# Two first copies given to VectorE, one feed-forward tile and one half tile moved in TensorE's order: a decoder layer on one Trainium2 core

## The chip, the cores and the metric

The kernel runs on one core of one Trainium2 chip. The metric is the device time of one execution in microseconds. TensorE is called PE here, VectorE DVE, ScalarE ACT, GpSimd POOL, and SyncE, which only issues transfers, SP. Each of them takes its instructions from its own queue, in order.

## The reference, cut to what matters

One decoder layer over 512 positions of width 1024: a norm, a combined projection, two attention branches merged by gates, an output projection, and then the part that this change touches, a second norm and a feed-forward block:

```
merged = gates[:, :, 0] * (y_a @ w_branch_a[l]) + gates[:, :, 1] * (y_b @ w_branch_b[l])
x = x + merged @ w_out[l]
h2 = rmsnorm(x, mlp_norm_g[l])
x = x + jnp.square(jax.nn.relu(h2 @ w_ff1[l])) @ w_ff2[l]      # w_ff1 1024x4096, w_ff2 4096x1024
return rmsnorm(x, final_norm_g)
```

## The kernel before

Each float32 product is made of three matmuls on PE: both operands are split into a high part (hi, ACT copies it, rounded) and the rest (lo, DVE or POOL subtracts), and hi·hi, hi·lo and lo·hi are added up in PSUM (`mm3`, L141 to L143). So each operand tile costs an ACT copy and then a subtraction, and the third matmul of a product needs the lo part of the left-hand tile.

Only PE's order is written out by hand. The order on ACT, DVE, POOL and SP comes from a scheduler that places each instruction by its own model of when its inputs are there. What the program text says about these four engines is therefore not yet their order.

**Start.** 52 tiny matmuls (`NWARM`, L160) run while the first inputs are loaded.

**Norm and start of the feed-forward.** The output projection (`out_proj`) goes over four blocks b of 128 positions. For each, the normed block xg is turned by eight PE transpositions (L875) and split by ACT (h2h, L876) and DVE (h2l, L877); that is `h2_block(b)`. For the last block, PE first runs the first halves (positions 0 to 255) of the tiles `ff1(0)` to `ff1(2)`, 24 matmuls each, then `h2_block(3)`, then the second halves. At the end of the transpositions the memory of the norm's tiles comes free, and the tiles that the second feed-forward product loads into (B, T) lie there.

**Feed-forward.** `ff1(f)` is one tile of 128 hidden units: 24 matmuls of 512 columns into a PSUM tile pt (two buffers), then ACT relu (z, L913) and square (z, L914). The second product goes in 8 groups g of four such tiles. Groups 0 to 6 multiply 2x2 block matrices by Strassen's scheme in Winograd's form, with 7 products per group (k = 0 to 6). `pair(g, k)` is one product, 2 x 6 matmuls on PE. Its left operand `as` is made by `put_a` (hi on ACT L953, lo on DVE L954) from the z tiles or from their sums S1 to S4 (DVE, L939). Its right operand `b` is made by `put_b` (hi on ACT L961, lo on DVE L962) from a loaded block (B11, B21, B22: `raw`, L923) or from a sum of blocks (T1 to T4: `tsum`). A T is loaded by SP (L928), and then POOL issues a second transfer that adds another block onto it (L929). T1 and T3 add a block from the weights, T2 adds T3 (so it waits for T3's landing), and T4 adds T2. The weights of ff1 tiles are loaded into `wraw` (L112) and split into whi (ACT, L119) and wlo (DVE, L121).

The products go to accumulators: `acc` (DVE, L985 or L983), and U and V, which collect products 0 and 2. In group 0 U and V have no contents yet and are copied from PSUM (L989), afterwards added to (L991). The order of PE in group 0 is ff1(3), ff1(4), pair(0,0), pair(0,1), ff1(5), pair(0,2), pair(0,3), pair(0,4), ff1(6), and so on; ff1(3) gives the second half of z1, the left operand of pair(0,1). The four PSUM tiles pl are used in turn, so pair(0,4) writes into those that pair(0,2) filled.

**End.** Group 7 is a plain product. In group 6 (`plain`), `last_put(j)` makes its left operand `al` (L999 on ACT, L1000 on DVE), `last_sums` joins U, V and acc, and `gfin`, the final norm's gains, is loaded into o (L1182 on SP) and scaled by ACT (L1183).

Of the kernel before, what the change touches and what calls it, by code (L numbers as in the profile page):

```python
# [14 lines left out]
AF = mybir.ActivationFunctionType  # L15
# [27 lines left out]
    return ap.to_broadcast(shape)  # L43


NWARM = 52
OHB = 12


def body(nc, tc, ctx, a, out, dbg=lambda name, ap: None):  # L50
    pe, dve, act, pool, sp = nc.tensor, nc.vector, nc.scalar, nc.gpsimd, nc.sync
# [19 lines left out]
    def utile(i, dt, name):  # L71
        return u_p.tile([128, 4, S], dt, tag=f"u{i}", name=name)
# [8 lines left out]
    def pa_tile():  # L81
        return psA.tile([128, S], F32, tag="pa", name="pa")

    def pl_tile():
        return psL.tile([128, S], F32, tag="pl", name="pl")

    def pt_tile():
        return psT.tile([128, NB, 128], F32, tag="pt", name="pt")
# [43 lines left out]
    def use(key, ahead=2):  # L132
        i = seq.index(key)
        for k in seq[i:i + ahead + 1]:
            pre(k)
        return W[key]

    def mm3(ps, parts):
        n = len(parts)
        for i, (lh, ll, rh, rl) in enumerate(parts):  # L140
            pe.matmul(ps, lh, rh, start=(i == 0), stop=False)  # L141
            pe.matmul(ps, lh, rl, start=False, stop=False)  # L142
            pe.matmul(ps, ll, rh, start=False, stop=(i == n - 1))  # L143
# [14 lines left out]
    pw = pa_tile()  # L158
    for _ in range(NWARM):
        pe.matmul(pw[:, 0:128], warmb, warmb, start=True, stop=True)  # L160
# [10 lines left out]
    k = 0  # L171
# [157 lines left out]
    for j in range(3):  # L329
# [9 lines left out]
        if j == 1:  # L339
# [12 lines left out]
            for j in range(2):  # L352
                t = t_p.tile([128, S], F32, tag="s2k", name="iqf", bufs=4)
# [155 lines left out]
    for b in range(NB):  # L509
        sl = slice(b * 128, (b + 1) * 128)  # L510
        for e in range(2):
            p = pl_tile()[:, :384]
# [40 lines left out]
    for j in range(4):  # L553
# [3 lines left out]
        p = pl_tile()  # L557
        cs = slice(128 * j, 128 * j + 128)
        mm3(p, [(ukh[:, cs], ukl[:, cs], zkh, zkl)])
        t = t_p.tile([128, S], F32, tag="s2k", name="kf", bufs=4)  # L560
# [10 lines left out]
        p = pl_tile()  # L571
# [75 lines left out]
    for t in range(0, 32 + BL, 2):  # L647
# [5 lines left out]
        h1, j = divmod(t - BL, 4)  # L653
# [161 lines left out]
    for m in range(NK):  # L815
# [4 lines left out]
        for br in (1, 0):  # L820
            yh, yl = (yah, yal) if br == 0 else (ybh, ybl)
            p = pl_tile()
# [47 lines left out]
    def h2_block(b):  # L870
        tk = slice(b * 128, (b + 1) * 128)
        for e in range(2):
            pt = pt_tile()
            for k in range(4):
                pe.transpose(pt[:, k], xg[b][:, (4 * e + k) * 128:(4 * e + k + 1) * 128], ident)  # L875
            act.activation(h2h.t[e][:, :, tk], pt, AF.Copy)  # L876
            dve.tensor_tensor(h2l.t[e][:, :, tk], pt, h2h.t[e][:, :, tk].bitcast(F32), op=ALU.subtract)  # L877
# [21 lines left out]
    def ff1_mm(p, f, lo=0, hi=S):  # L899
        wh_, wl_ = W["ff1", f]  # L900
        mm3(p[:, lo:hi], [(wh_[:, k], wl_[:, k], h2h[k][:, lo:hi], h2l[k][:, lo:hi]) for k in range(NK)])

    def ff1(f, p=None):
        g, i = divmod(f, 4)
        j, q = divmod(i, 2)
        if p is None:
            use(("ff1", f), min(2, 31 - f))
            p = pt_tile().rearrange("p a b -> p (a b)")
            ff1_mm(p, f)
        if q == 0:  # L910
            Z[g, j] = z_p.tile([128, 2, S], F32, tag=f"z{j}", name=f"z{j}", bufs=1)
        z = Z[g, j][:, q]
        act.activation(z, p, AF.Relu)  # L913
        act.activation(z, z, AF.Square)  # L914
# [6 lines left out]
    def raw(g, key):  # L921
        r = RAW[g, key] = wt_p.tile([128, 2, 512], F32, tag="raw", name=key, bufs=3)
        sp.dma_start(r, wsrc(g, key))  # L923

    def tsum(g, key):
        t = TT[g, key] = wt_p.tile([128, 2, 512], F32, tag="t", name=key, bufs=3)
        x, y = {"T1": ("B11", "B12"), "T3": ("B12", "B22"), "T2": ("B11", "T3"), "T4": ("B21", "T2")}[key]
        sp.dma_start(t, wsrc(g, x))  # L928
        pool.dma_start(t, TT[g, y] if y[0] == "T" else wsrc(g, y), accum_op=ALU.add)  # L929

    def asum(g, key):
        z0, z1 = Z[g, 0], Z[g, 1]
        t0, t1 = slice(0, 256), slice(256, 512)
        x, y, op = {"S1": (z0[:, :, t1], z1[:, :, t1], ALU.subtract),
                    "S2": (SS.get((g, "S1")), z0[:, :, t0], ALU.subtract),
                    "S3": (z0[:, :, t0], z0[:, :, t1], ALU.subtract),
                    "S4": (z1[:, :, t0], SS.get((g, "S2")), ALU.add)}[key]
        t = SS[g, key] = z_p.tile([128, 2, 256], F32, tag="s", name=key, bufs=3)
        dve.tensor_tensor(t, x, y, op=op)  # L939
# [17 lines left out]
    def put_b(g, k):  # L957
        key = ORDER[k][1] if g < NG - 1 else LASTB[k]
        x = (RAW if key[0] == "B" else TT)[g, key]
        t = bs_p.tile([128, 2, 2, 512], F32R, tag="b", name="b", bufs=NBS)  # L960
        act.activation(t[:, 0], x, AF.Copy)  # L961
        dve.tensor_tensor(t[:, 1], x, t[:, 0].bitcast(F32), op=ALU.subtract)  # L962
        BS[g, k] = (t[:, 0], t[:, 1])
# [3 lines left out]
    copied = {}  # L967

    def unit(g, k, m, cuts=(0, 512)):
        p = pl_tile()  # L970
        ah, al = AS[g, "op", k]
        bh, bl = BS[g, k]
        ms = slice(m * 128, (m + 1) * 128)
        for lo, hi in zip(cuts, cuts[1:]):
            c = slice(lo, hi)
            mm3(p[:, c], [(ah[:, q, ms], al[:, q, ms], bh[:, q, c], bl[:, q, c]) for q in range(2)])
            i, n = BLOCK.get(k, (0, 0))
            b = 2 * i + m
            cs = slice(512 * n + lo, 512 * n + hi)
            if k in BLOCK:  # L980
                t = acc[:, b, cs]
                if k == 5:
                    dve.tensor_tensor(t, t, p[:, c], op=ALU.subtract)  # L983
                else:
                    dve.tensor_tensor(t, p[:, c], t, op=ALU.add)  # L985
            t = {0: U, 2: V, 3: U}.get(k)
            if t is not None:
                if g == 0 and k != 3:
                    copied[k] = act.activation(t[:, m], p, AF.Copy)  # L989
                else:  # L990
                    dve.tensor_tensor(t[:, m], p[:, c], t[:, m], op=ALU.add)  # L991

# [3 lines left out]
    def last_put(j):  # L996
        t = utile(j, F32R, "al")
        hi, lo = t[:, 0:2], t[:, 2:4]
        act.activation(hi, Z[NG - 1, j], AF.Copy)  # L999
        dve.tensor_tensor(lo, Z[NG - 1, j], hi.bitcast(F32), op=ALU.subtract)  # L1000
        AS[j] = (hi, lo)
# [25 lines left out]
    def pair(g, k):  # L1027
        for m in range(2):
            unit(g, k, m)
# [3 lines left out]
    def group(g):  # L1033
        nxt = g + 1
        plain = nxt == NG - 1

        def nb():
            if bq:
                put_b(*bq.pop(0))

        def raws():
            for key in ("B11", "B21", "B12" if plain else "B22"):
                raw(nxt, key)

        if g == 0:
            put_a(g, 2)
            asum(g, "S4")
            ff1(4 * nxt)
            nb()
            tsum(0, "T4")  # L1050
            pair(g, 0)
            put_a(g, 3)
            pair(g, 1)
            with tc.issue_after(copied[0].ins):
                nb()
            put_a(g, 4)
            ff1(4 * nxt + 1)
            put_a(nxt, 0)
            nb()
            pair(g, 2)  # L1060
            raws()
            nb()
            nb()
            for key in ("T1", "T3", "T2"):
                tsum(nxt, key)
        else:
            pair(g, 0)
            raws()
            put_a(g, 2)
            asum(g, "S4")  # L1070
            ff1(4 * nxt)
            nb()
            pair(g, 1)
            nb()
            if not plain:
                for key in ("T1", "T3", "T2"):
                    tsum(nxt, key)
            put_a(g, 3)
            pair(g, 2)
            nb()  # L1080
            put_a(g, 4)
            ff1(4 * nxt + 1)
            if not plain:
                put_a(nxt, 0)
        put_a(g, 5)
        pair(g, 3)
        nb()
        put_a(g, 6)
        pair(g, 4)
        nb()  # L1090
        if plain:
            raw(nxt, "B22")
        else:
            tsum(nxt, "T4")
        ff1(4 * nxt + 2)
        if plain:
            last_put(0)
        pair(g, 5)
        nb()
        ff1(4 * nxt + 3)  # L1100
        if not plain:
            asum(nxt, "S1")
            asum(nxt, "S2")
        pair(g, 6)
        nb()
        if plain:
            last_put(1)
            last_sums()
        else:
            asum(nxt, "S3")  # L1110
            put_a(nxt, 1)
# [33 lines left out]
    for j in range(3):  # L1145
        use(("ff1", j), 2 - j)
        p0.append(pl_tile())
        ff1_mm(p0[j], j, 0, 256)
    h2_block(3)
    for j in range(3):  # L1150
        ff1_mm(p0[j], j, 256, S)
    m_st.close()
# [23 lines left out]
    for g in range(NG - 1):  # L1176
        group(g)
# [54 lines left out]
```

## Time and profile before

| what | value |
|---|---|
| time, median of 3 runs (lowest to highest) | 707.0 us (706.18 to 708.35) |
| time of the profiled execution | 708.5 us |
| its span in the trace | 706.8 us |
| PE busy | 689.6 us, 98% of the span |
| DVE, ACT, POOL busy | 72%, 51%, 27% |

The profiled execution's own time is 1.7 us above its span, which is what lies around the traced instructions, and 1.5 us above the median. Times in rows are microseconds from the start of the span. In a row of the timeline the first number is the start, the second the duration, then engine, line, operation, tiles and shape; in brackets at the end stands the idle time of that engine before the row, and what ended it. Matmuls overlap, so their pace is read from start to start.

### The profile page before, as it was taken

Reading aid. Unit: us, or ns where it says so; the run is one execution under the profiler, and the core shown is the slowest. Engines: PE = TensorE matmul, PEld = TensorE weight load, DVE = VectorE, ACT = ScalarE, POOL = GpSimd, SP = SyncE. Lnnn points to the kernel's source line nnn. Section 1 sums busy time; section 2 is a strip of 40 time slices with the busy share of each in tenths; the row PEclk is TensorE's granted clock in tenths of the full one; section 3 lists DMA queues with packets and bytes.
Section 4 is the critical chain, followed back from the end, with each engine's and each line's share of the span. In section 5 each row is a group of like instructions: output and inputs, shape, how many; then the busy total and the mean of one; then the engine's idle time right before and its main releaser. Section 6 shows DMA issues by size and latency. Waiting matters only on the chain.

```text
span 706.8 us, 10176 instructions
## 1 busy us (share of the span) xinstructions
PE 689.6 (98%) x3671; PEld 557.7 (79%) x3672; DVE 509.5 (72%) x936; ACT 360.9 (51%) x623; POOL 191.0 (27%) x235
## 2 busy tenths in 40 slices
PE   9999999999999999999999979999999999999996
PEld 7879788768865777888889768888888888888875
DVE  6487899999999765674323856958595776859643
ACT  6466767654735445761114755454354535444333
POOL 2305387665156540230011010101010011000132
PEclk9999999999999999999999999999999999999999
DMA  8632532112221117972009896878768786750012
GB/s 309 239 112 91 125 116 80 46 46 79 101 75 45 47 47 285 309 270 89 0 1 309 221 258 188 220 227 196 195 181 213 174 215 184 196 120 30 31 49 101
DMA packets 41587, 102.88 MB, mean 146 GB/s; under 512 B 4352, under 2 KB 5248, under 8 KB 41536
## 3 DMA queue, kind: packets, MB, share of 16 engines
q1 hardware_dynamic: 34848, 86.47, 36.1%
q0 software_dynamic: 5824, 14.68, 12.1%
q10 hardware_dynamic: 864, 1.08, 0.4%
q8 instruction: 29, 0.48, 0.3%
q14 instruction: 22, 0.18, 0.1%
HBM read 87.66 MB, written 6.29 MB: 133 GB/s over the span
## 4 chain that ended last, share of the span: by engine, by line
PE 77%; DVE 12%; DMA 5%; issue 2%; ACT 2%; POOL 1%; SPq 0%; POOLq 0%; ACTq 0%; DVEq 0%
PE pl L141 10%; PE pl L143 10%; PE pl L142 10%; PE pt L142 7%; PE pt L141 7%; PE pt L143 7%; PE pl L237 3%; PE pl L239 3%; PE pl L238 3%; DVE nmx L590 2%; DVE oh L714 2%; DMA T<-T 2%; PE pl L848 2%; PE pl L846 2%; PE pl L847 2%
## 5 line engine op out<-in xcount | busy, mean ns | idle before, releaser
L119 ACT ACTIVATE whi<-wraw 128x1024 fp32r<-128x1024 f32 (+1 forms) x71 | 74.6, 1051 | 92.4 <-PE pt L142 74.3
L121 DVE TENSOR_TENSOR wlo<-wraw,whi 128x1024 fp32r<-128x1024 f32 (+1 forms) x60 | 73.7, 1230 | 53.0 <-ACT whi L119 52.1
L141 PE MATMUL pt<-h2h,whi 128*128 128x512 f32 x232 | 90.3, 389 | 0.0
L142 PE MATMUL pt<-h2l,whi 128*128 128x512 f32 x232 | 90.3, 389 | 0.0
L143 PE MATMUL pt<-h2h,wlo 128*128 128x512 f32 x232 | 90.2, 389 | 0.0
L141 PE MATMUL pl<-b,as 128*128 128x512 f32 x196 | 77.3, 394 | 3.7 <-ACT V L989 3.7
L143 PE MATMUL pl<-b,as 128*128 128x512 f32 x196 | 76.8, 392 | 0.1
L142 PE MATMUL pl<-b,as 128*128 128x512 f32 x196 | 76.9, 392 | 0.0
L962 DVE TENSOR_TENSOR b<-T,b 128x1024 fp32r<-128x1024 f32 x28 | 34.2, 1221 | 28.3 <-ACT b L961 28.3
L961 ACT ACTIVATE b<-T 128x1024 fp32r<-128x1024 f32 x28 | 29.6, 1057 | 42.5 <-PE pl L143 15.3
L142 PEld LDWEIGHTS pt<-h2l,whi 128*128 128x128 f32 x232 | 43.6, 188 | 9.1
L141 PEld LDWEIGHTS pt<-h2h,whi 128*128 128x128 f32 x232 | 43.5, 188 | 9.0
L143 PEld LDWEIGHTS pt<-h2h,wlo 128*128 128x128 f32 x232 | 43.5, 188 | 9.0
L929 POOL DMA_DIRECT2D T<-wff x14 | 17.2, 1244 | 116.6 <-DVE V L991 40.0
L714 DVE TENSOR_SCALAR oh<-posbc,thr 128x400 bf16<-128x400 f32 (+31 forms) x128 | 45.6, 408 | 3.9 <-PE pl L735 3.9
L141 PEld LDWEIGHTS pl<-b,as 128*128 128x128 f32 x196 | 37.2, 190 | 12.1 <-ACT V L989 4.2
L237 PE MATMUL pl<-hh,whi 128*128 128x512 f32 x112 | 44.8, 400 | 0.0
L595 POOL TENSOR_SCALAR pra<-pra,rs 128x400 f32<-128x400 f32 (+31 forms) x32 | 35.1, 1109 | 35.2 <-DVE rs L594 35.1
L239 PE MATMUL pl<-hh,wlo 128*128 128x512 f32 x112 | 43.7, 390 | 0.0
L238 PE MATMUL pl<-hl,whi 128*128 128x512 f32 x112 | 43.7, 390 | 0.0
L143 PEld LDWEIGHTS pl<-b,as 128*128 128x128 f32 x196 | 37.1, 189 | 8.2 <-DVE as L954 0.5
L142 PEld LDWEIGHTS pl<-b,as 128*128 128x128 f32 x196 | 37.2, 190 | 8.1 <-DVE b L962 0.4
(324 smaller groups left out, 1683.7 us busy)
## 6 DMA issues: line engine op xcount, KB each, us to landing
wraw<-wff SPq DMA_DIRECT2D x32, 512.0 KB, 4.3
T<-wff SPq DMA_DIRECT2D x28, 512.0 KB, 4.6
B<-wff SPq DMA_DIRECT2D x25, 512.0 KB, 6.4
wraw<-wF SPq DMA_DIRECT2D x24, 512.0 KB, 3.3
T<-wff POOLq DMA_DIRECT2D x14, 512.0 KB, 8.8
T<-T POOLq DMA_DIRECT2D x14, 512.0 KB, 5.7
gd<-gt SPq DMA_DIRECT2D x16, 256.0 KB, 2.2
wraw<-wbr SPq DMA_DIRECT2D x8, 512.0 KB, 4.2
```

Of the source, the lines that this page charges most:

```text
L119: act.activation(hi, raw, AF.Copy)
L121: eng.tensor_tensor(lo, raw, hi.bitcast(F32), op=ALU.subtract)
L141: pe.matmul(ps, lh, rh, start=(i == 0), stop=False)
L142: pe.matmul(ps, lh, rl, start=False, stop=False)
L143: pe.matmul(ps, ll, rh, start=False, stop=(i == n - 1))
L237: pe.matmul(p, h[:, k], hh[k], start=(k == 0), stop=False)
L238: pe.matmul(p, h[:, k], hl[k], start=False, stop=False)
L239: pe.matmul(p, l[:, k], hh[k], start=False, stop=(k == NK - 1))
L595: pool.tensor_scalar(pr, pr, rs, None, op0=ALU.mult)
L714: dve.tensor_scalar(oh[:, :n], posbc[:, :n], thr[:, 4 * G + q:4 * G + q + 1], None, op0=ALU.is_le)
L961: act.activation(t[:, 0], x, AF.Copy)
L962: dve.tensor_tensor(t[:, 1], x, t[:, 0].bitcast(F32), op=ALU.subtract)
```

## The change

It has four parts. `NWARM` goes from 52 to 46. The copies of the first contents of U and V (L989 of before) go from ACT to DVE. In group 6, ff1(31) and `last_put(1)` stand ahead of pair(6,5); before, ff1(31) stood behind that pair and `last_put(1)` behind pair(6,6). And `h2_block(3)` stands ahead of the first half of ff1(2), no longer behind it.

```diff
-NWARM = 52
+NWARM = 46
@@ unit
                 if g == 0 and k != 3:
-                    copied[k] = act.activation(t[:, m], p, AF.Copy)
+                    copied[k] = dve.tensor_copy(t[:, m], p)
                 else:
                     dve.tensor_tensor(t[:, m], p[:, c], t[:, m], op=ALU.add)
@@ group
         ff1(4 * nxt + 2)
         if plain:
             last_put(0)
+            ff1(4 * nxt + 3)
+            last_put(1)
         pair(g, 5)
         nb()
-        ff1(4 * nxt + 3)
         if not plain:
+            ff1(4 * nxt + 3)
             asum(nxt, "S1")
             asum(nxt, "S2")
         pair(g, 6)
         nb()
         if plain:
-            last_put(1)
             last_sums()
         else:
             asum(nxt, "S3")
@@ body
     for j in range(3):
         use(("ff1", j), 2 - j)
         p0.append(pl_tile())
+        if j == 2:
+            h2_block(3)
         ff1_mm(p0[j], j, 0, 256)
-    h2_block(3)
     for j in range(3):
         ff1_mm(p0[j], j, 256, S)
```

The scheduler's order moves more than these lines say. In the lists below a number behind a tile's name is its buffer; the same tile has a number lower by 6 in the changed kernel.

**ACT, from the first T of group 0 on.** Before: `pt_4653` is ff1(3)'s result, `z1_4632` the tile that pair(0,1) multiplies by way of `as_4629`, and T2's copy stands far below, behind the two copies of U.

```order
L961 ACTIVATE b_4733<-T1_4615 128x1024
L119 ACTIVATE whi_4701<-wraw_4699 128x1024
L913 ACTIVATE z1_4632<-pt_4653 128x512
L914 ACTIVATE z1_4632<-z1_4632 128x512
L953 ACTIVATE as_4629<-z1_4632 128x512
...
L989 ACTIVATE U_4606<-pl_4739 128x512
L989 ACTIVATE U_4606<-pl_4748 128x512
L961 ACTIVATE b_4775<-T2_4621 128x1024
```

Now, with `pt_4647` the result of ff1(3) and `as_4623` pair(0,1)'s operand:

```order
L961 ACTIVATE b_4727<-T1_4609 128x1024
L914 ACTIVATE z1_4626<-z1_4626 128x512
L961 ACTIVATE b_4769<-T2_4615 128x1024
L913 ACTIVATE z1_4626<-pt_4647 128x512
L119 ACTIVATE whi_4695<-wraw_4693 128x1024
L914 ACTIVATE z1_4626<-z1_4626 128x512
L961 ACTIVATE b_4811<-B22_4607 128x1024
L953 ACTIVATE as_4623<-z1_4626 128x512
```

T2's copy has moved from behind group 0's first copies of U to a place ahead of the relu of ff1(3), and B22's copy to a place ahead of the operand of pair(0,1).

**DVE, in the same stretch.** Before:

```order
L962 TENSOR_TENSOR b_4733<-T1_4615,b_4733 128x1024
L121 TENSOR_TENSOR wlo_4702<-wraw_4699,whi_4701 128x1024
L939 TENSOR_TENSOR S1_4686<-z0_4624,z1_4632 128x512
L954 TENSOR_TENSOR as_4629<-z1_4632,as_4629 128x512
```

Now:

```order
L962 TENSOR_TENSOR b_4727<-T1_4609,b_4727 128x1024
L121 TENSOR_TENSOR wlo_4696<-wraw_4693,whi_4695 128x1024
L939 TENSOR_TENSOR S1_4680<-z0_4618,z1_4626 128x512
L962 TENSOR_TENSOR b_4811<-B22_4607,b_4811 128x1024
L939 TENSOR_TENSOR S2_4682<-S1_4680,z0_4618 128x512
L939 TENSOR_TENSOR S3_4684<-z0_4618 128x512
L954 TENSOR_TENSOR as_4623<-z1_4626,as_4623 128x512
```

B22's lo part and the sums S2 and S3 now stand ahead of the lo part of pair(0,1)'s operand.

**SP, the loads around T4's base.** Before:

```order
L923 DMA B21_4838<-wff2 128x2x512
L928 DMA T4_4736<-wff2 128x2x512
L112 DMA wraw_4903<-wff1 128x1024
L112 DMA wraw_4956<-wff1 128x1024
L112 DMA wraw_5045<-wff1 128x1024
L112 DMA wraw_5134<-wff1 128x1024
```

Now:

```order
L923 DMA B21_4832<-wff2 128x2x512
L112 DMA wraw_4897<-wff1 128x1024
L928 DMA T4_4730<-wff2 128x2x512
L112 DMA wraw_4950<-wff1 128x1024
L112 DMA wraw_5039<-wff1 128x1024
L923 DMA B22_4834<-wff2 128x2x512
```

One load of ff1 weights stands ahead of T4's base now, where it waits only for wlo_4638, the lo part of ff1(4)'s weights. The load into wraw_5039 waits for wlo_4696, which stands behind T2's copy.

## Rows read from the trace of the kernel before

**Rows 1.** The head of the page: span, and busy time of each engine.

```profile
span 706.8 us, 10176 instructions
PE 689.6 (98%) x3671; PEld 557.7 (79%) x3672; DVE 509.5 (72%) x936; ACT 360.9 (51%) x623; POOL 191.0 (27%) x235
```

**Rows 2.** The waits of PE: tile and line that waited, what released it, total us, times, longest.

```profile
PE pl L141 <- ACT V L989: 3.7, 1, 3.7
PE pl L143 <- DVE al L1000: 1.4, 1, 1.4
...
PE pl L188 <- ACT hh L182: 0.6, 1, 0.6
...
PE pl L142 <- DVE h2l L877: 0.3, 1, 0.3
PE pl L141 <- ACT h2h L876: 0.2, 1, 0.2
```

**Rows 3.** Timeline of PE: the last matmul of pair(0,3), the first of pair(0,4), and the first of ff1(6).

```profile
407.13 0.39 PE L143 MATMUL pl<-b,as 128*128 128x512 f32 x1
411.26 0.79 PE L141 MATMUL pl<-b,as 128*128 128x512 f32 x1 [3.75 <-ACT V L989]
...
415.62 0.39 PE L141 MATMUL pt<-h2h,whi 128*128 128x512 f32 x1
```

**Rows 4.** Windows of 4 us around that wait; the number behind POOL's is the granted clock of PE as a share of full speed.

```profile
408.00:412.00 4.00, 0.74 (x2) 0.64 (x3) 2.60 (x3) 3.97 (x7) 0.14 (x1) 0.89 0.72 242
412.00:416.00 4.00, 4.00 (x14) 3.17 (x13) 3.86 (x5) 2.11 (x3) 1.92 (x2) 0.69 0.98 338
```

**Rows 5.** Timeline of ACT up to the first copy of V; the first row is the copy of T4.

```profile
407.58 1.06 ACT L961 ACTIVATE b<-T 128x1024 fp32r<-128x1024 f32 x1 [2.27 <-PE pl L143]
408.54 1.04 ACT L119 ACTIVATE whi<-wraw 128x1024 fp32r<-128x1024 f32 x1
...
410.10 0.63 ACT L914 ACTIVATE z<-z 128x512 f32<-128x512 f32 x1
410.63 0.58 ACT L989 ACTIVATE V<-pl 128x512 f32<-128x512 f32 x1
```

**Rows 6.** The chain that ended last, its three transfers in group 0: start, us, what. They are the adds of T3, T2 and T4.

```profile
380.82 10.79 DMA T<-wff
...
391.91 10.42 DMA T<-T
...
402.97 4.52 DMA T<-T
```

**Rows 7.** Timeline of PE: first matmul of pair(0,0), then the first and the third of pair(0,1).

```profile
390.24 0.39 PE L141 MATMUL pl<-b,as 128*128 128x512 f32 x1
...
392.98 0.50 PE L141 MATMUL pl<-b,as 128*128 128x512 f32 x1
...
393.82 0.50 PE L143 MATMUL pl<-b,as 128*128 128x512 f32 x1
```

**Rows 8.** Timeline of ACT in the same stretch; the first row is the copy of T1, the last is pair(0,1)'s operand with one more behind it.

```profile
389.11 1.06 ACT L961 ACTIVATE b<-T 128x1024 fp32r<-128x1024 f32 x1 [6.94 <-DMA T<-wff]
390.07 1.05 ACT L119 ACTIVATE whi<-wraw 128x1024 fp32r<-128x1024 f32 x1
391.02 0.58 ACT L913 ACTIVATE z<-pt 128x512 f32<-128x512 f32 x1
391.63 0.64 ACT L914 ACTIVATE z<-z 128x512 f32<-128x512 f32 x1
392.30 1.15 ACT L953 ACTIVATE as<-z 128x512 fp32r<-128x512 f32 x2
```

**Rows 9.** Timeline of DVE in the same stretch.

```profile
390.20 1.23 DVE L962 TENSOR_TENSOR b<-T,b 128x1024 fp32r<-128x1024 f32 x1 [7.29 <-ACT b L961]
391.34 1.22 DVE L121 TENSOR_TENSOR wlo<-wraw,whi 128x1024 fp32r<-128x1024 f32 x1
392.48 0.69 DVE L939 TENSOR_TENSOR S<-z,z 128x512 f32<-128x512 f32 x1
393.08 0.68 DVE L954 TENSOR_TENSOR as<-z,as 128x512 fp32r<-128x512 f32 x1
```

**Rows 10.** Timelines of PE and SP: the first matmul of the third first half, the eight transpositions of the norm's last block, and the first loads behind them.

```profile
365.83 0.28 PE L141 MATMUL pl<-h2h,whi 128*128 128x256 f32 x1
...
368.71 1.04 PE L875 MATMUL pt<-ident,xg 128*128 128x128 f32 x8
...
369.89 1.40 SPq L923 DMA_DIRECT2D B<-wff  x3
```

**Rows 11.** The transfer queues in the window 380 to 384 us: what all queues moved, and the only queue listed (q1 is that of SP's transfers, q0 that of POOL's).

```profile
DMA packets 446, 1.09 MB, mean 272 GB/s; under 512 B 27, under 2 KB 27, under 8 KB 446
q1 hardware_dynamic: 446, 1.09, 98.4%
```

**Rows 12.** The same in the window 392 to 396 us.

```profile
q1 hardware_dynamic: 325, 0.74, 79.4%
```

**Rows 13.** Timelines of ACT and DVE at the end: the scaling of the final gains, and the lo part of the last `al`.

```profile
675.02 1.06 ACT L1183 ACTIVATE o<-o 128x1024 f32<-128x1024 f32 x1 [0.21 <-DMA o<-gfin]
...
677.73 2.35 DVE L1000 TENSOR_TENSOR al<-z,al 128x1024 fp32r<-128x1024 f32 x1
```

**Rows 14.** Timeline of PE at the start: the 52 warm-up matmuls.

```profile
1.08 4.89 PE L160 MATMUL pa<-warmb 128*128 128x128 bf16 x52 [1.08 <-DVE warmb L157]
```

## The prediction

> **What bounds the kernel now.** The page comes first: PE is busy for 98% of the span, no other engine for more than 72% [rows 1]. So time can be won only where PE waits, and lost where it is made to wait. The waits of PE name the places: 3.7 us once for the first copy of V, 1.4 us once for the lo part of the last `al`, 0.6 us at the start, and 0.3 and 0.2 us around the norm's last block [rows 2]. Each of the change's four parts touches one of them.
>
> The timeline prices the largest. pair(0,3) gives out its last matmul at 407.13, and at the usual pace the next would stand 0.23 us later; pair(0,4) starts at 411.26, so 3.9 us pass idle [rows 3]. The idle time has a second price: the granted clock is 0.89 and 0.69 in the windows behind it, so part of them ran at the half level (1.2 GHz) [rows 4], and the twelve matmuls of pair(0,4) take from 411.26 to 415.62, 4.36 us [rows 3], where those of pair(0,0) take from 390.24 to 392.98, 2.74 us [rows 7]. That is 1.6 us more, 5.5 us in all.
>
> ACT's rows show why V was late: its copy (410.63) stands behind T4's copy, which starts at 407.58 [rows 5], when the chain's third transfer, issued at 402.97, has landed 4.52 us later. That transfer hung on T2's add (391.91, 10.42 us), and this on T3's (380.82, 10.79 us) [rows 6]. So the feed-forward starts with three transfers in a row, and whatever stands behind one of them in a queue inherits its lateness. This is what I look for in the changed order.
>
> **The copies of U and V.** Four copies go from ACT to DVE. V's still stand behind T4's lo part there, but that has landed some 10 us ahead of pair(0,2)'s end by the shift below, so the wait of rows 3 goes: **−5.5 us**. The copies themselves cost DVE four times about 0.60, the distance between two of its instructions of 512 columns (392.48 to 393.08) [rows 9]; DVE has 28% free, and the cover is PE's ff1(5) and ff1(6).
>
> But the reordering behind this part has a price. T2's copy now stands on ACT directly ahead of the relu of ff1(3). Before, this relu ran at 391.02, and pair(0,1)'s operand came out of it in time for 392.98, with PE never waiting [rows 7, 8]. ACT takes its queue in order: now the relu waits until T2 has landed. Before, that was at 391.91 + 10.42 = 402.3 [rows 6], 9 us behind the time when pair(0,1) should start. Behind the waiting copy stand the relu, a weight copy, the square, B22's copy and the operand; who waits for the operand is PE.
>
> Call T2's landing L. From L, ACT needs 0.96 to the relu (the step 389.11 to 390.07), 0.48 for it (half of that for half the columns), 0.95 for whi (390.07 to 391.02), 0.53 for the square (410.10 to 410.63), 0.95 for B22 [rows 5, 8]: the operand starts at L + 3.87, and PE 0.68 later, as 392.98 followed 392.30: L + 4.55 [rows 7, 8]. DVE sets the third matmul, which needs the lo part: wlo starts 1.1 behind whi's start (389.11 to 390.20), at L + 2.5, then 1.14, 0.60, 1.14, 0.60, 0.60 for wlo, S1, B22's lo, S2 and S3 by the steps of rows 9, so lo starts at L + 6.6, and the third matmul 0.74 later (393.08 to 393.82): **L + 7.35** [rows 7, 9].
>
> **When T2 lands.** The norm's part moves 24 matmuls of 0.12 us behind the transpositions, so these stand where the third half tile did: 365.83 and not 368.71, 2.88 us earlier [rows 10]. The loads that start behind them (369.89) and the POOL adds follow. Against it, one more weight load of 0.52 MB stands ahead: at 272 GB/s [rows 11] 1.9 us. T3's add, which ended at 380.82 + 10.79 = 391.6 [rows 6], ends between 388.7 (the extra load costs nothing) and 390.6; T2's add is issued 0.3 us later, as before. Its own length lies between 4.52 us, the shortest of the three adds (T4's), and 10.42, that of T2's itself [rows 6], with T4's base and three weight loads queued beside it by SP's order. Now T4's base and one weight load are beside it, since the next waits for wlo behind T2's copy. I take the middle, 7.5. With 390.9 for the issue, L = 398.4; the ends are 388.7 + 0.3 + 4.5 = 393.5 and 390.9 + 10.4 = 401.3.
>
> So the third matmul of pair(0,1) comes at 398.4 + 7.35 = 405.7 in place of 393.82: **+11.9 us** (ends +7.0 and +14.8). What the norm's part wins on PE itself (0.5 us of waits [rows 2], behind a half tile of 2.88 us) is swallowed: PE only waits for T2 sooner. After some 11 us idle the clock will fall as it did after 3.75 us; I charge the same **+1.6 us** (nothing, if the first two matmuls and the wait for lo cover it; twice that, if it stays low longer).
>
> Later transfers do not add to it. T1's base of the next group waits for T2's lo and comes some 2 to 3 us later, while PE is 7 us later.
>
> **The last tile.** ff1(31) starts one pair, 2.7 us, earlier, and its `al` is made beside pair(6,5). In front on ACT remains the scaling of the final gains (675.02), whose load hangs on ff1(31) too and moves with it. The lo part began at 677.73 and took 2.35 us [rows 13]; 2.7 earlier, and without the wait for POOL's sums, it ends about 2 us ahead of its use. So the 1.4 us of rows 2 go: **−1.4**.
>
> **The warm-ups.** 52 take 4.89 us [rows 14], six about 0.5. The first product isn't held by them alone: 0.6 us further on PE waits for `hh` [rows 2], which hangs on a load. What the six give back, that wait takes: 0, at most −0.5.
>
> **Sum.** +11.9 + 1.6 − 5.5 − 1.4 = +6.6 us. From the profiled execution's 708.5 this gives 715.1, with a span of 713.4; that execution lay 1.5 above the median, so the forecast is **713.6 us**.
>
> **Rivals.** First, *the adds get their share of the engines at once.* The Trainium skill says so ("DMA: Bandwidth & Descriptors", Queues, rings and completion order): each DMA engine round-robins between the queues it has work for, packet by packet. By rows the mechanism is this: two adds issued at about 377 and 378, with an equal share for SP's queue, are 2.1 MB at 272 GB/s [rows 11], 7.7 us, so T3 lands near 385.6; T2's add then has 0.52 MB and an equal share, 3.8 us and a microsecond to start, so L is 390.7. The third matmul comes at 398.0, +4.2 us; the sum is 4.2 + 1.6 − 5.5 − 1.4 = −1.1, or 705.9: no change. Against it, POOL's queue isn't even listed between 380 and 384, where both adds had been issued and SP's queue took 98.4%, and between 392 and 396 SP's queue took 79.4% and POOL's again nothing [rows 11, 12]. By that rule the adds would have shown there; the trace disagrees. Chance 0.08.
>
> Second, *faster*: T2's copy does not hold ACT, since T2 has landed when ACT comes to it. Below L = 385.4 (third matmul not behind 393.82 − 1.1) nothing is lost, and the gains remain: 5.5 + 1.4 + 0.5 = 7.4, 699.6. It decides at L = 389.9: there the stall costs 3.4 + 1.6, and the sum is −1.9. For that, T3 would have to land by 385.1, 6.5 us sooner than before, while the loads ahead start 2.9 sooner and are one more. Chance 0.05.
>
> Third, *worse*: T2's add is as slow as before, because the weight load and T4's base go ahead of it whole. L = 401.3, +9.5 us in sum, 716.5; if the last `al` waits on besides, because the gains' load holds ACT, 717.9. For it speaks that POOL's queue moved nothing while T4's base did [rows 12]; against it, that two of the loads behind are gone. Chance 0.17.
>
> Fourth, the copies of V on DVE come late again and pair(0,4) waits: the −5.5 would fall away. PE comes to it 7 us or more later than before, T4 hardly later, so I count it in the third.
>
> **How the numbers follow.** The forecast has the remaining 0.70. The range goes from the low end of L (+7.0 + 1.6 − 6.9 = +1.7, 708.7) to the third rival with its addition and rounded in, 709 to 717.5. A measurement of this kernel can tell about 0.3%, 2.1 us, from no change: slower by more 0.87 (forecast and third rival), within it 0.08, faster 0.05.
>
> **What the next profile would show.** Right: ACT idle for about 10 us ahead of a copy b<-T and the relu z<-pt right behind it; PE waiting in pair(0,1), L141 for `as` of L953 and L143 for `as` of L954, 13 us in all from about 392; a granted clock under 1 behind it; no wait for V, none for `al`; the first loads of B at 367. Wrong: T2's add under 4 us or issued by 386; pair(0,4) still waiting; or the new stall there, but PE's loss given back because a later wait of the old kernel was only hidden.

## The result, and the profile after

The changed kernel takes 712.9 us (median of 6 runs, 712.2 to 714.5) against 707.3 (median of 6 runs of the kernel before): a ratio of 1.0079, 95% interval 1.0062 to 1.0097. It is 5.5 us slower; 713.6 was forecast. Its profiled execution took 712.2 us with a span of 710.5. That is only 3.7 above the span of before, since this execution lies 0.7 below its median and that of before lay above its own. The terms below are compared between the two traces, so their sum is to be held against 3.7.

The waits of PE, and the head of the page, answer to [rows 1, 2]:

```profile
span 710.5 us, 10170 instructions
PE 688.9 (97%) x3665; PEld 558.0 (79%) x3666; DVE 512.4 (72%) x940; ACT 359.1 (51%) x619; POOL 191.9 (27%) x235
...
PE pl L141 <- ACT as L953: 8.7, 1, 8.7
PE pl L143 <- DVE as L954: 1.6, 1, 1.6
...
PE pl L188 <- ACT hh L182: 0.9, 1, 0.9
```

The waits for V, for the last `al` and for the norm's split are gone, and a new one of 8.7 + 1.6 us stands in pair(0,1). The timeline of ACT shows where it comes from (compare [rows 8]):

```profile
386.10 1.06 ACT L961 ACTIVATE b<-T 128x1024 fp32r<-128x1024 f32 x1 [6.43 <-DMA T<-wff]
387.07 0.61 ACT L914 ACTIVATE z<-z 128x512 f32<-128x512 f32 x1
395.84 1.06 ACT L961 ACTIVATE b<-T 128x1024 fp32r<-128x1024 f32 x1 [8.16 <-DMA T<-T]
396.80 0.58 ACT L913 ACTIVATE z<-pt 128x512 f32<-128x512 f32 x1
397.28 1.05 ACT L119 ACTIVATE whi<-wraw 128x1024 fp32r<-128x1024 f32 x1
398.22 0.62 ACT L914 ACTIVATE z<-z 128x512 f32<-128x512 f32 x1
398.74 1.04 ACT L961 ACTIVATE b<-B 128x1024 fp32r<-128x1024 f32 x1
399.69 0.62 ACT L953 ACTIVATE as<-z 128x512 fp32r<-128x512 f32 x1
```

ACT stands still for 8.2 us ahead of T2's copy, with the relu of ff1(3) right behind it, although PE had given out that tile's last matmul by 383.3 (24 matmuls of 0.23 us ahead of 388.79, where pair(0,0) begins). The chain that ended last runs through the two adds and then through exactly the instructions that the forecast lists ahead of the lo part:

```profile
378.14 12.02 DMA T<-wff
390.16 0.29 issue
390.45 5.36 DMA T<-T
...
396.80 0.58 ACT z L913
397.38 0.95 ACT whi L119
...
398.35 0.55 DVE wlo L121
...
399.50 0.68 DVE S L939
400.18 1.14 DVE b L962
401.32 1.20 DVE S L939 x2
402.52 0.61 DVE as L954
```

PE's timeline and the windows (compare [rows 3, 4, 7]): the last matmul of pair(0,0), the first, third and fourth of pair(0,1), the first of ff1(5).

```profile
391.29 0.39 PE L143 MATMUL pl<-b,as 128*128 128x512 f32 x1
400.36 0.79 PE L141 MATMUL pl<-b,as 128*128 128x512 f32 x1 [8.68 <-ACT as L953]
...
403.18 0.79 PE L143 MATMUL pl<-b,as 128*128 128x512 f32 x1 [1.60 <-DVE as L954]
403.77 0.63 PE L141 MATMUL pl<-b,as 128*128 128x512 f32 x1
...
407.48 0.40 PE L141 MATMUL pt<-h2h,whi 128*128 128x512 f32 x1
...
396.00:400.00 4.00, 0.00 (x0) 0.00 (x0) 1.65 (x2) 4.00 (x6) 0.85 (x1) 0.50 0.60 115
404.00:408.00 4.00, 4.00 (x12) 3.09 (x12) 4.00 (x8) 2.14 (x4) 0.00 (x0) 0.59 0.21 78
```

Behind the wait the granted clock is 0.50 and 0.59, so PE ran at its lower level (1.2 GHz) until it came to ff1(5).

At the end, the rows that answer to [rows 13] (ACT's scaling of the gains, DVE's lo part of the last `al`), and PE's first and third matmul of the last group:

```profile
677.58 1.06 ACT L1185 ACTIVATE o<-o 128x1024 f32<-128x1024 f32 x1
680.30 1.22 DVE L1000 TENSOR_TENSOR al<-z,al 128x1024 fp32r<-128x1024 f32 x1
682.21 0.39 PE L141 MATMUL pl<-b,al 128*128 128x512 f32 x1
682.67 0.39 PE L143 MATMUL pl<-b,al 128*128 128x512 f32 x1
```

The lo part of the last `al` is ready at 681.5, and no matmul waits for it: the last group has its last matmul 21.8 us behind its first, where it took 23.5 before.

### The profile page after: what moved, and what is told of

It reads as the page before. It is cut to its first block, busy times and chain, and to the rows that moved or that the text cites. A ratio compares the mean times of both kernels' runs of the same rounds, so it can differ in the third digit from the quotient of the medians.

```text
span 710.5 us, 10170 instructions
## 1 busy us (share of the span) xinstructions
PE 688.9 (97%) x3665; PEld 558.0 (79%) x3666; DVE 512.4 (72%) x940; ACT 359.1 (51%) x619; POOL 191.9 (27%) x235
## 4 chain that ended last, share of the span: by engine, by line
PE 80%; DVE 13%; DMA 3%; issue 2%; ACT 1%; POOL 1%; SPq 0%; POOLq 0%; DVEq 0%; ACTq 0%
PE pl L143 11%; PE pl L141 11%; PE pl L142 11%; PE pt L141 7%; PE pt L142 7%; PE pt L143 7%; PE pl L237 3%; PE pl L239 3%; PE pl L238 3%; DVE nmx L590 2%; DVE oh L714 2%; PE pl L848 2%; PE pl L846 2%; PE pl L847 2%; DVE sc L401 2%; DVE m L400 2%
```

## The experiments

The theory to be tested: the loss is the place of T2's copy in ACT's queue, and what the change moved there. Its rivals: the norm's new order with its extra weight load; DVE with four more copies; the transfers themselves, whatever the order. All ratios are to the kernel before, run beside, with 95% intervals.

**The copies alone, and everything but the copies.** `only_copies` is the kernel before with the one line of the copies changed; `acts_copies` is the changed kernel with that line put back.

```diff
-                    copied[k] = act.activation(t[:, m], p, AF.Copy)
+                    copied[k] = dve.tensor_copy(t[:, m], p)
```

> The kernel before with the four copies on DVE and nothing else of the change. In the order T2's copy then stands behind the relu and the square, but still ahead of the operand of pair(0,1). Theory: PE waits there from 393.0 until T2's landing plus 2.3 us; T3 lands at 391.6, T2's add takes between 5.4 us (as in the changed kernel) and 10.4 (as before), so the third matmul of pair(0,1) comes between 399.6 and 404.6, 5.8 to 10.8 us late; with 2.0 for the half clock and V's wait of 5.8 gone, the time is 2 to 7 us above the kernel before (ratio 1.003 to 1.010). Rival (the norm's new order makes the loss, the copies alone win V's wait): ratio 0.992, no wait in pair(0,1).

Measured: 1.0081 (1.0067 to 1.0095), the whole loss of the change, with the norm's order untouched. PE waits in pair(0,1), and on ACT T2's copy stands directly ahead of the operand:

```profile
PE pl L141 <- ACT as L953: 9.9, 1, 9.9
...
400.49 1.06 ACT L961 ACTIVATE b<-T 128x1024 fp32r<-128x1024 f32 x1 [9.57 <-DMA T<-T]
401.45 0.61 ACT L953 ACTIVATE as<-z 128x512 fp32r<-128x512 f32 x1
```

> The whole change without the copies: U's and V's first copies stay on ACT. Theory: no wait in pair(0,1); 0.3 at the start, 1.1 at the norm and 1.7 at the end are won; V's copies still stand behind T4's on ACT, which lands between 401 and 406 (407.5 before) since the loads start 3.2 us earlier, so the wait in pair(0,4) is between nothing and 3.4 us: 3 to 9 us faster than before, ratio 0.987 to 0.996. Rival (the norm's new order makes the loss): a wait of 5 us or more in group 0 and a ratio of 1.00 or above.

Measured: 0.9958 (0.9945 to 0.9972), 3.0 us faster. The wait for V is still there, shorter than the 3.7 of before because T4 lands 2.9 us earlier (404.6 for 407.5):

```profile
PE pl L141 <- ACT V L989: 2.8, 1, 2.8
```

So the copies alone cost as much as the whole change, and the 3.0 us that the three other parts win are lost beside them. T2 lands 4.6 us sooner in the changed kernel (395.8 for 400.5). T3's add lands at the same time in both (390.2 and 390.3); it is T2's own add that is shorter there, 5.4 us for 9.9, with one weight load beside it and not three. But in the changed kernel more stands between T2's copy and the operand, and ff1(5) starts at 407.5 in the one and 407.4 in the other, so the shorter add and the longer queue behind it cancel. The norm's order as the cause is out.

**Which engine copies V.** In `u_on_act` only U's two copies go back to ACT.

```diff
-                    copied[k] = dve.tensor_copy(t[:, m], p)
+                    copied[k] = act.activation(t[:, m], p, AF.Copy) if k == 0 else dve.tensor_copy(t[:, m], p)
```

> The whole change, but the two first copies of U stay on ACT; V's go to DVE. T2's copy then stands behind them on ACT again, and with it behind the relu of ff1(3) and the operand of pair(0,1). Theory (the T2 copy ahead of that relu makes the whole loss): no wait above 0.5 us in pair(0,1), pair(0,0) starts at 388.8 as in the changed kernel, and the gains remain: 0.3 at the start, 1.1 at the norm, 5.8 at V, 1.7 at the end, 8.9 us in all, a span near 698 and a ratio near 0.988 to the kernel before; if V's copies on DVE still have to wait behind T4's lo part, up to 2 us less gain. Rival (the norm's new order, with the weight load it puts ahead of the adds, or V's copies on DVE, make the loss): pair(0,1) or pair(0,4) waits 5 us or more and the ratio is 1.00 or above.

Measured: 0.9956 (0.9943 to 0.9968), where 0.988 was expected. There is no wait in pair(0,1), so T2's copy behind the relu removes the loss; but instead of the gain at V there is this:

```profile
PE pl L141 <- DVE V L989: 2.7, 1, 2.7
```

2.7 us with V copied by DVE, 2.8 with V copied by ACT: moving V's copies is worth nothing. They stand behind T4's copy on ACT and behind its lo part on DVE, and T4 lands at 403.4 here, when pair(0,4) is due at about 405. In the changed kernel V's wait was gone because PE came there 13 us later (418.4: twelve matmuls ahead of ff1(6), 421.1), not because another engine did the work.

Why U's copies decide this can be read in the program. Both kernels tie T2's `put_b` behind U's first copy (the line with `copied[0]` below). With that copy on ACT, T2's copy stands behind it in ACT's order, before and in `u_on_act` (there U's at 395.5, T2's at 398.3); with it on DVE, T2's copy stands ahead of pair(0,1)'s operand, in the changed kernel and in `only_copies`. So the tie held on ACT only as long as the instruction that it names ran there.

**T2's copy tied behind the operand, copies on DVE.** `t2_behind` has the whole change, with T2's `put_b` placed behind the ACT copy of pair(0,1)'s operand (the line that notes this copy in `copied` is left out here).

```diff
-            with tc.issue_after(copied[0].ins):
+            with tc.issue_after(copied["as", 0, 1].ins):
                 nb()
```

> The whole change, all four copies on DVE; only T2's put_b is tied behind the ACT copy of pair(0,1)'s operand instead of behind U's first copy. Theory: as the run with U on ACT, no wait above 0.5 us in pair(0,1), ratio near 0.988 (0.985 to 0.992). Rival (four more copies load DVE so that the lo parts in group 0 come late): a wait of PE for a DVE tile in group 0 of 2 us or more, and a ratio at least 0.004 above that of the run with U on ACT.

Measured: 1.0054 (1.0040 to 1.0067), far from 0.988. There is no wait in pair(0,1), but two others, and DVE's row shows what made the first:

```profile
PE pl L141 <- DVE U L989: 4.9, 1, 4.9
PE pl L141 <- DVE V L989: 2.9, 1, 2.9
...
400.58 1.29 DVE L954 TENSOR_TENSOR as<-S,as 128x512 fp32r<-128x512 f32 x2 [8.54 <-ACT as L953]
```

On ACT the operands S1 and S2 now stand behind T2's copy, on DVE their lo parts stand ahead of U's copies, and so these wait for T2 by way of two engines. By its signs the rival came true (waits for DVE tiles of 4.9 and 2.9 us, a ratio 0.0098 above that of `u_on_act`), but its cause, DVE's load, is not what the row shows: DVE is idle for 8.5 us. The theory was too narrow, since it named one instruction behind the copy.

**V ahead of T4.** `v_first` keeps the three other parts, leaves the copies on ACT, and ties T4's `put_b` behind V's copies; `v_first_alone` is the kernel before with that tie alone.

```diff
             nb()
-            nb()
+            with tc.issue_after(copied[2].ins):
+                nb()
```

> The whole change without the copies on DVE (U's and V's first copies on ACT), and T4's put_b tied behind V's copies, so that on ACT and DVE nothing that pair(0,4) waits for stands behind a copy of T4. Theory (what stands behind the copies of T2 and T4 in a queue makes the waits of group 0, whichever engine copies U and V): no wait above 0.3 us in group 0, the granted clock 1.00 in every window from 388 to 420, pair(0,4) at 405.5; against the run with the copies on ACT it wins 2.8 us of wait and 1.8 of half clock, 4.5 in all: ratio 0.989 (0.987 to 0.992). Rival (the copies load ACT, so only moving them away helps): the wait for V stays at 1 us or more.

> The kernel before with one edit: T4's put_b tied behind V's copies. Theory: the wait for V (3.9 us with the step to the next matmul) and its half clock (1.7) go and nothing else moves: 5.6 us faster, ratio 0.992 (0.990 to 0.994). Rival (V's copy would be late anyway, or the next thing in line waits for T4): a wait of 1 us or more in pair(0,4) to pair(0,6), ratio above 0.995.

Measured: 0.9985 (0.9972 to 0.9998) and 1.0024 (1.0013 to 1.0036), neither as expected. Group 0 behaved as foretold in `v_first`, at a granted clock of 1.00 from 388 to 424; the wait came back one group later, in pair(1,1) (in `v_first_alone` 2.3 + 1.6 us, with 0.4 us left for V). PE and then ACT of `v_first`:

```profile
435.23 0.76 PE L141 MATMUL pl<-b,as 128*128 128x512 f32 x1 [3.03 <-ACT as L953]
437.54 0.80 PE L143 MATMUL pl<-b,as 128*128 128x512 f32 x1 [1.12 <-DVE as L954]
...
430.42 1.06 ACT L961 ACTIVATE b<-T 128x1024 fp32r<-128x1024 f32 x1 [8.61 <-DMA T<-T]
431.39 1.04 ACT L119 ACTIVATE whi<-wraw 128x1024 fp32r<-128x1024 f32 x1
432.34 0.58 ACT L913 ACTIVATE z<-pt 128x512 f32<-128x512 f32 x1
```

It is the same picture: in group 1 the relu of ff1(7) stands behind T2's copy. In the kernel before that cost nothing, because PE came late enough, held by V in group 0. The price of 3.0 + 1.1 us and the half clock behind it is more than V's wait had been.

**Every T2 tied behind the operand.** `t_late` adds to `v_first`, for all later groups:

```diff
         pair(g, 6)
-        nb()
         if plain:
+            nb()
             last_sums()
         else:
             asum(nxt, "S3")
             put_a(nxt, 1)
+            with tc.issue_after(copied["as", nxt, 1].ins):
+                nb()
```

> The whole change without the copies on DVE, T4's put_b of group 0 tied behind V's copies as in the run v_first, and in every later group T2's put_b tied behind the ACT copy of the operand of pair(g,1). Theory (whatever PE waits for and stands behind a copy of T2 or T4 in ACT's queue waits for that transfer, in group 1 as in group 0): the waits that v_first still has in group 1 (3.0 and 1.1 us, and some 3 us of half clock) go, none above 1 us takes their place in groups 0 to 2, and against v_first about 7 us are won: ratio 0.988 (0.985 to 0.991), the fastest of all. Rival (the transfers themselves bound group 1, whatever the order): a wait of 2 us or more in group 1 or 2 stays and the ratio is 0.995 or above.

Measured: 0.9877 (0.9862 to 0.9893), 699.5 us against 708.1 beside it, the fastest of all. Span and the largest wait that is left in the feed-forward:

```profile
span 698.2 us, 10162 instructions
...
PE pl L143 <- DVE as L954: 0.3, 1, 0.3
```

The transfers land about when they did in `v_first`: in group 0 T2 at 398.5 for 399.1 and T4 at 403.7 for 404.3, in group 1 T2 at 430.8 for 430.3. Only what stood behind their copies moved. So the transfers did not bound group 1, the order did.

**The same with the copies on DVE.** `t_late_dve` is the changed kernel, copies on DVE, with the ties added and T2's moved further back.

```diff
-            with tc.issue_after(copied[0].ins):
-                nb()
             put_a(g, 4)
+            with tc.issue_after(copied[0].ins), tc.issue_after(copied["as", 0, 4].ins):
+                nb()
```

> The changed kernel with all its four copies on DVE, and only ties added: T2's put_b of group 0 behind the ACT copies of the operands of pairs 3 and 4, T4's behind V's copies, T2's of every later group behind the operand of pair(g,1). Theory (the loss is the place of the copies of T2 and T4 in the queues, and which engine copies U and V is worth nothing): as the run t_late, no wait above 0.5 us in groups 0 and 1, ratio 0.988 (0.985 to 0.991). Rival (copies on DVE cost or gain by themselves): a ratio that differs from t_late's 0.9877 by more than 0.003.

Measured: 0.9944 (0.9930 to 0.9957); neither 0.988 nor clear evidence on the engine, since one wait was left, 2.9 us for V. ACT, then DVE:

```profile
404.41 1.06 ACT L961 ACTIVATE b<-T 128x1024 fp32r<-128x1024 f32 x1 [2.26 <-DMA T<-T]
405.37 1.04 ACT L119 ACTIVATE whi<-wraw 128x1024 fp32r<-128x1024 f32 x1
...
406.44 1.23 DVE L121 TENSOR_TENSOR wlo<-wraw,whi 128x1024 fp32r<-128x1024 f32 x1 [2.07 <-ACT whi L119]
407.58 0.68 DVE L989 COPY V<-pl 128x512 f32<-128x512 f32 x1
```

A tie on the program's order of T4 did not keep T4's copy on ACT behind a copy on DVE. T4's copy holds a weight's whi on ACT, this holds wlo on DVE, and V's copy stands behind wlo. T2's copy was held by its second tie, to a copy on ACT; the tie to U's first copy alone had not held it in the changed kernel. That V on DVE is worth nothing rests on `u_on_act` against `acts_copies`; U's copies were not moved alone.

**What the half clock costs.** PE gets idle matmuls between pair(0,0) and pair(0,1) of the changed kernel, 36 of them (`keep_busy`) or 52 (`keep_busy_52`); nobody reads their results.

```diff
             pair(g, 0)
+            pw2 = pa_tile()
+            (fh, _), (fb, _) = AS[0, "op", 0], BS[0, 0]
+            for _ in range(52):
+                pe.matmul(pw2, fh[:, 0, 0:128], fb[:, 0, :], start=True, stop=True)
```

> The changed kernel with 36 more matmuls of 512 columns on PE between pair(0,0) and pair(0,1), whose results nobody reads; at 0.227 us each they fill 8.2 of the 8.7 us in which PE waits. They cost no time on the path, which hangs on T2's landing. If the half clock behind the wait comes from the idle time, the granted clock stays 1.00 from 388 to 404 and pair(0,1) runs its ten last matmuls in 2.3 instead of 4.3 us: 2.0 us off the changed kernel, a span of 708.5 and a ratio to the kernel before of 1.005. If the clock falls for another reason, the ratio stays at 1.008 and the clock at 0.5 to 0.6 in 400 to 408.

> The changed kernel with 52 instead of 36 idle matmuls of 512 columns between pair(0,0) and pair(0,1): 11.8 us at 0.227, from 391 to 403, where the operand came at 400.4 and its lo part at 403.2 in the changed kernel (at 402.8 and 405.6 in the run with 36, whose T2 add took longer). If the half clock comes from idle time: granted clock 1.00 until 404 and after, the ten last matmuls of pair(0,1) 0.227 us apart, 2.0 us less than in the changed kernel behind the same landing of T2. If not: 0.427 us apart though PE was never idle for more than 3 us.

With 36, 1.0088 (1.0065 to 1.0111): inconclusive. T2's add took 9.0 us in that trace and not 5.4, so PE ran out of idle matmuls, waited 3.4 and 2.1 us, and fell to half clock all the same. With 52, 1.0054 (1.0035 to 1.0072), and the trace settles it: the add took 5.6 us, the granted clock is 1.00 throughout, and pair(0,1) needs 2.7 us from its first matmul to ff1(5):

```profile
391.48 11.95 PE L1055 MATMUL pa<-b,as 128*128 128x512 f32 x52
403.26 0.39 PE L141 MATMUL pl<-b,as 128*128 128x512 f32 x1
...
405.98 0.39 PE L141 MATMUL pt<-h2h,whi 128*128 128x512 f32 x1
400.00:404.00 4.00, 4.00 (x20) 3.30 (x19) 4.00 (x6) 4.00 (x8) 0.00 (x0) 1.00 0.71 193
```

ff1(5) starts 1.5 us earlier than in the changed kernel, though the idle matmuls held the third matmul until 403.7, half a microsecond longer. The half clock therefore came from the idle time and cost 2.0 us.

**The norm's part and the end's part alone.** `only_norm` and `only_last` are the kernel before with one of these moves each, as in the change's diff.

> The kernel before with the norm's last transpositions ahead of the third first half, and nothing else. The relu of ff1(3) stays ahead of T2's copy. Theory: PE comes to group 0 1.1 us earlier, which the wait for V swallows; the loads start 2.9 us earlier, one more weight load stands ahead and one fewer beside T2's add, T4 lands near 404.6 instead of 407.5 as in the run without the copies, and V's copy with it: 2 to 3 us faster, ratio 0.996 to 0.9975, the wait for V still 2.5 to 3 us. Rival (the transfers don't start earlier, or the extra load takes it back): ratio 0.999 or above.

Measured: 0.9964 (0.9951 to 0.9977), 2.5 us. The mechanism holds in kind: T4 lands at 405.5 for 407.5. It is 0.9 later than expected, and the wait for V is 3.6, so the gain came by way of the loads and the PE time won at the norm went into that wait.

> The kernel before with the move of the last ff1 tile and its last_put alone. Theory: the wait of PE for the last al (1.4 us in the waits, 1.7 from the last group's first matmul to its last in the changed kernel) goes and nothing else moves: ratio 0.9976 (0.996 to 0.999). Rival: the scaling of the final gains or B22's lo part takes its place: ratio 1.000.

Measured: 0.9987 (0.9978 to 0.9996), 0.9 us; the wait for `al` is gone from the trace. That is at the lower end of what was expected. Together the two make 3.4 us where `acts_copies`, with the warm-ups, made 3.0.

## Why the prediction was right, point by point

**The stall.** Right in its place, cause and length behind the landing: the third matmul of pair(0,1) comes at 403.18, 7.37 us behind T2's landing at 395.81, where 7.35 was worked out from single steps of rows.

**The landing** was the term most off: 395.8, not 398.4. T3's add landed at 390.16 (390.6 was foretold), but T2's add took 5.36 us where the middle, 7.5, was taken; the range of 4.5 to 10.4 held it. The stall so cost 9.4 us in place of 11.9.

**The half clock** cost 2.0 us (ten matmuls from 403.18 to 407.48 in 4.30 and not 2.27), where 1.6 was charged.

**V.** The first matmul of ff1(6) stands 5.5 us later than before, that of ff1(5) 11.3 later (407.48 for 396.22): 5.8 us were given back, 5.5 foretold. The forecast credited this to T4's lo part being ready some 10 us ahead of pair(0,2)'s end "by the shift below", and `u_on_act` shows how much hung on that clause: without the stall the same copies on DVE wait 2.7 us. The fourth rival was therefore the true price of this part wherever PE is on time; the forecast folded it into the third and gave it no time of its own.

**The end** gave 1.7 us back where 1.4 was foretold, in the traces; alone it measured 0.9 (0.3 to 1.6). **The norm and the start** moved pair(0,0) from 390.24 to 388.79, and that went into the wait as said. Not all of these 1.45 us belong to the change: with the old norm and start pair(0,0) began between 389.3 and 390.4 in four traces, with the new ones between 388.3 and 389.1 in nine, so some 1.1 on average. `only_norm`, with 52 warm-ups, began at 389.0; what the six warm-ups gave back can't be told from the spread.

**Sum, in the traces:** +9.4 + 2.0 − 5.8 − 1.7 = +3.9, against 3.7 between the spans. Foretold was +6.6; 2.1 of the difference is T2's add. The median moved by 5.5, more than the profiled pair; that other executions had longer adds is possible, as `keep_busy` and `keep_busy_52` differ by 3.4 us in this one transfer, but their landings were not seen. That 713.6 came so near to 712.9 is therefore in part luck: by the traces' terms the forecast was 2.7 us too high.

**What the forecast did not name** is why the order changed: the tie to U's first copy, which no longer held T2's copy on ACT. It read the consequence off the new order.

**The rivals.** *Shares at once* did not come: its time was 705.9. Its mechanism is half there, however. In the changed kernel's trace POOL's queue took 32.4% between 379 and 383 us beside 68.7% of SP's; between 390.5 and 392.5, right behind the issue of T2's add, it took nothing. The Trainium skill's rule ("DMA: Bandwidth & Descriptors", Queues, rings and completion order) agrees with the first window. The second doesn't speak against it: that rule of the Trainium skill is about queues that have work, and the trace doesn't show from when the packets of an issued add stand ready. The forecast took the silence of POOL's queue as evidence against the rule, and that was too much: in the trace before, right behind its window of 380 to 384, POOL's queue took 52.6% and SP's 54.4% between 384 and 386. *Faster* needed L, T2's landing, below 389.9, and L was 395.8. *Worse*, an add as slow as before, did not come in the changed kernel's trace (5.4 us); `only_copies`, with the old order of the loads, has one of 9.9.

## What to carry to other kernels

An engine's queue is in order, so a copy that waits for a late transfer delays everything behind it, and a wait can pass through two engines before it reaches the busy one; read the scheduler's order for what stands behind each such copy, and tie the copy behind the work that the busy engine needs next. A wait that is removed early in a chain may only uncover the same wait one stage later: here the tie at V paid nothing until T2's copy was tied back in every later group, and both together, with the three other parts, made the kernel 1.2% faster than before, where the three parts alone made 0.4%. Before work is moved to another engine, ask what it waits for there, and whether an ordering tie names it: the tie may then no longer hold on the engine that it was written for; a gain that rests on another stall is none.

## What was not expected of the hardware

The same transfer, T2's add of 0.5 MB in group 0, took between 5.4 and 10.5 us in the fourteen traces, and the loads that SP had issued around it (counted up to 2 us behind its issue) go with its length. With T4's base and one weight load beside it: 5.4 and 5.6 us (changed kernel, `keep_busy_52`), but 9.0 (`keep_busy`) where the base was issued only 0.3 us ahead of the add and not about 2. With two weight loads and the base about 2 us ahead: 8.4 to 9.2 in six runs. With the base less than a microsecond ahead and two or three weight loads: 9.9 to 10.5. T4's add, later, took 4.5 us in all but one trace (5.1 in `only_copies`). The number of loads and the lead of the base were not varied by themselves, so which of them sets the length stays open.
